# Convolution input in two DRAM tensors and started a group earlier, LayerNorm in four stages, attention's norm weight in the output weights

## The chip, the cores and the metric

The kernel runs on one core of a Trainium2 chip. The metric is the device time of one execution in microseconds (us), the median over runs.

## The reference

Two layers of a diffusion backbone over 256 prompt tokens and 1024 sample tokens (ten tiles of 128 tokens, width 1024). Each layer: RMSNorm with a modulation, one input projection, two branches of "heads", one output projection, a second RMSNorm, a gated residual. The change touches layer 0 alone (`even_mix`), of which this is the core:

```python
a_u, a_g, a_z, b_q, b_k, b_v, b_z = jnp.split(h @ w_in, SPLIT_E, axis=-1)
a = a_u * jax.nn.sigmoid(a_g)
a = lax.conv_general_dilated(a, conv_w[:, None, :], window_strides=(1,),
        padding=[(15, 15)], feature_group_count=A_W) + conv_b        # 512 channels, 31 taps
a = jax.nn.silu(layer_norm(a, ln_g, ln_b)) * jax.nn.silu(a_z)
...
o = over_query_blocks(lambda qb: diff_attend(qb, keys, vals, lam), q)  # softmax 1 - lam * softmax 2
o = rms_norm(o, subln_g) * (1.0 - lam_init)
o = o.reshape(b, T, B_W) * jax.nn.silu(b_z)
return jnp.concatenate([a, o], axis=-1) @ w_out, new_kv
```

## The kernel before, in words

**Layer 0's input part** (`l0_in`) is a list of seven groups of projections: ug0 and ug1 (each 256 channels of a_u and a_g), az, and head 0 to head 3 (q, k, v and z of one head of attention). A group has 10 units (one tile of tokens each) or, for a head, 14; TensorE does a unit as matmuls in three parts, of high and low halves, over eight chunks of weights `w_w`. In the last batch of a group (three or four units together) the next group's weights are loaded, cast on ScalarE (L269) and split on GpSimd (L270).

After every unit a `filler` advances a second piece of work by some steps: `cv`, which is the convolution followed by LayerNorm, and `mod`, the modulation vectors. Before, the groups from az on advance `cv` by one step a unit, and by two at every third. `cv` is a generator: `conv()` has 66 steps, which read the convolution's input back from DRAM in eight blocks of 64 channels (`windows`, tile `X`) and multiply it on TensorE by banded tap matrices (`band`; `tr_cv`, L471), with evictions on ScalarE (L476) and VectorE (L477); `ln_steps()` has six more, two tiles of tokens a step but for the first: load, statistics on VectorE (L574 to L581, with the root on GpSimd, L95), normalisation on ScalarE (L582) and GpSimd (L583, L584), tanh on ScalarE (L585), two multiplies on VectorE (L586, L587), store (L588). What is left of `cv` when the last group ends is run out after it.

In the heads, `ch_done` rotates q and k (sum on GpSimd L499, then L500 on ScalarE and L501 on VectorE), `vz_done` makes v and the gate `gz`: silu (L339, L340), then a multiply with `subg`, the norm weight of attention times 0.4 on every row (L513), and the store (L514). `split_stack` makes the prompt tokens' q and k (`hl`, L357; transposed on TensorE as `tr_st`, L360).

**Between input part and attention**, at a place in head 3 (`freed0`), keys of head 0 (`l0_keys`: loads `kd`, `ck`, subtractions on GpSimd L653) and the queries of its token group 1 (`l0_query`: `qs`, four loads) are loaded ahead.

**Attention** (`l0_attn`) takes for each head five groups of two tiles: scores S on TensorE (L777), row maximum and softmax (`row_softmax`: L394 on VectorE, the exponential L397 on ScalarE), two of them for each head. Their weighted difference: L784 and L785 make the weight `wc`, L787 (VectorE, first 1024 columns) and L789, L790 (GpSimd, the others) the difference E; then transposes, splits and the product with V. `fin` squares and sums the transposed output (L718 on ScalarE), adds the EPS term (L719, L720 on VectorE), takes the root (L95 on GpSimd) and multiplies by root and gate into `oy` (L724).

**Output projection**: `wo_chunk` loads a chunk of 128 rows of the output weights (`wor`, L815), casts it (ScalarE, L818) and splits it (GpSimd, L819); of eight chunks the last four belong to attention.

A scheduler puts the instructions in order when the kernel is built, by its own estimates; on the chip each engine then runs its list in that order, and the DMA issues of SP stand in one such list, too.

Of the kernel before, what the change touches and what calls it, by code (L numbers as in the profile page):

```python
# [76 lines left out]
class K:  # L77
# [323 lines left out]
    def l0_in(self, ws, raw, wp, cxp, p1, small, acc, pst, mod, freed):  # L401
# [4 lines left out]
        for hl in range(2):  # L406
            for r0, r1 in ((0, 15), (271, CW0 + 15), (CW0 + 15 + 1024, CROWS)):
                nc.sync.dma_start(f32(self.AW[hl, r0:r1]), z0[0 : r1 - r0])

        def ug_units(gi):  # L410
            def done(t, ps):
# [7 lines left out]
                dst = self.AW[:, r : r + 128, gi * 256 : gi * 256 + 256]  # L419
# [63 lines left out]
        def head_units(h):  # L483
# [23 lines left out]
            def vz_done(t, ps):  # L507
# [49 lines left out]
        def ln_steps():  # L557

            con = cxp.tile([128, 3, 512], F32, tag="cy", bufs=1, name="lncon")
            for i, nm in enumerate(("lng", "lnb", "convb")):  # L560
# [2 lines left out]
            def load(p):
                w = cxp.tile([128, CWIN * CCH], F32, tag="X", bufs=2, name=f"lu{p}")
                w = w[:, 0:2560].rearrange("p (i c) -> p i c", c=512)
                az = small.tile([128, 512], F32, tag="az", bufs=2, name=f"azr{p}")
                for i in range(2):
                    r = (2 * p + i) * 128 + (0 if p < 1 else CW0 - 256)
                    nc.sync.dma_start(w[:, i], self.CV[r : r + 128])
                    nc.sync.dma_start(w[:, 4] if i else az, self.AZ[2 * p + i])  # L570
                return w, (az, w[:, 4])

            def tile(t, u, th, az):
# [11 lines left out]
                nc.scalar.activation(th, u, AF.Tanh, scale=0.5)  # L585
                nc.vector.scalar_tensor_tensor(u, th, 1.0, u, ALU.add, ALU.mult)  # L586
# [974 lines left out]
```

## Time and profile before

| | |
|---|---|
| runs | 1823.73, 1828.43, 1829.55 us (median 1828.43) |
| the profiled execution | 1829.68 us, span 1827.9 us |
| mean granted TensorE clock | 0.985 |
| TensorE (PE) busy | 1727.2 us, 94% of the span |
| VectorE (DVE) | 1238.3 us, 68% |
| ScalarE (ACT) | 971.6 us, 53% |
| GpSimd (POOL) | 782.0 us, 43% |

The time is that of the whole execution; the span is from the first to the last instruction that the profiler saw. Busy shares are averages over stages with different limits. Layer 0's input part runs to some 514 us, its attention to some 800 us; layer 1 follows. In the page's 40 slices of 45.7 us TensorE's granted clock is 0.9 or more in all but one, which holds the passage from the input part to attention (0.7), and the DMA engines are 70 to 80% busy between 91 and 183 us and again from 229 to 411 us or so, with dips.

### The profile page before, as it was taken

The page shows a single profiled execution, that of the slowest core. Times are in us where ns is not written, and L with a number is a line of the kernel's source. Part 1 is how long each engine was busy: PE and PEld are TensorE (multiplying, and loading weights), DVE is VectorE, ACT ScalarE, POOL GpSimd, SP SyncE. Part 2 cuts the span into 40 slices and gives each one's busy share as a digit, 9 for nine tenths or more (in the row PEclk, how much of TensorE's full clock was granted, in tenths as well). Part 3 has the DMA queues.
Part 4 walks back from the last instruction along what each step waited for, and adds up shares of the span by engine and source line. Part 5 has one row for each costly group of instructions (what it writes and reads, how often), then busy time and mean ns, then how long its engine had stood idle before and what let it go on. Part 6 is the DMA issues. An engine that isn't in the chain of part 4 may idle for free. (4 is left out here: it accounts for less than half of the span.)

```text
span 1827.9 us, 28289 instructions
## 1 busy us (share of the span) xinstructions
PE 1727.2 (94%) x9434; PEld 1419.5 (78%) x9434; DVE 1238.3 (68%) x2975; ACT 971.6 (53%) x2040; POOL 782.0 (43%) x696
## 2 busy tenths in 40 slices
PE   6999999999859999899999999998999999999998
PEld 2787788988747777778887778886888888878886
DVE  6657545674779999945566672118899989999322
ACT  6432244344337777753344543217778878898311
POOL 2322022222557777763237873203344334354332
PEclk9999999999979999999999999999999999999999
DMA  8457478785764433144146346254112114141441
GB/s 292 166 161 211 150 185 203 190 234 134 222 185 113 139 104 93 47 137 163 72 156 199 139 121 167 75 137 113 36 43 66 36 41 107 53 146 58 156 173 55
DMA packets 220086, 241.24 MB, mean 132 GB/s; under 512 B 72128, under 2 KB 154464, under 8 KB 219684
## 3 DMA queue, kind: packets, MB, share of 16 engines
q1 hardware_dynamic: 207284, 233.53, 43.1%
q0 software_dynamic: 1792, 3.15, 0.9%
q10 hardware_dynamic: 10864, 2.75, 0.8%
q8 instruction: 75, 1.23, 0.3%
q14 instruction: 71, 0.58, 0.1%
HBM read 169.08 MB, written 70.28 MB: 131 GB/s over the span
## 5 line engine op out<-in xcount | busy, mean ns | idle before, releaser
L397 ACT ACTIVATE E<-E,mm 128x1536 f32<-128x1536 f32 (+3 forms) x240 | 293.5, 1227 | 69.0 <-DVE E L394 58.4
L270 POOL TENSOR_TENSOR w_w<-raw_w,w_w 128x512 fp32r<-128x512 f32 x88 | 118.7, 1360 | 258.1 <-ACT w_w L269 244.0
L1217 PE MATMUL S<-k1d,q1s 128*128 128x512 f32 (+1 forms) x704 | 206.4, 389 | 4.5 <-DMA q1s<-qT 2.1
L372 POOL TENSOR_TENSOR el<-ef,eh 128x512 fp32r<-128x512 f32 x96 | 124.3, 1296 | 185.6 <-DVE eh L371 180.7
L394 DVE TENSOR_SCALAR_CACHE_REDUCE E<-S,mm 128x512 f32<-128x512 f32 x256 | 189.8, 744 | 11.5 <-PE S L777 3.0
L1147 PE MATMUL wt_et<-ident,E 128*128 128x128 f32 x1264 | 186.2, 273 | 3.2 <-ACT E L397 2.5
L1147 PEld LDWEIGHTS wt_et<-ident,E 128*128 128x128 f32 x1264 | 153.6, 140 | 37.3 <-ACT E L397 4.3
L777 PE MATMUL S<-kd,qs 128*128 128x512 f32 (+1 forms) x416 | 133.4, 431 | 30.2 <-DVE E L394 24.1
L368 DVE TENSOR_TENSOR el<-wt_et,eh 128x512 fp32r<-128x512 f32 x220 | 146.8, 682 | 10.0 <-ACT eh L367 9.3
L1217 PEld LDWEIGHTS S<-k1d,q1s 128*128 128x128 f32 x704 | 121.3, 190 | 28.5 <-DVE E L394 7.1
L367 ACT CAST eh<-wt_et 128x512 fp32r<-128x512 f32 x220 | 124.1, 594 | 30.4 <-PE wt_et L1147 29.9
L1142 PE MATMUL pv_pv<-el,v 128*128 128x512 f32 x316 | 138.8, 439 | 0.5 <-POOL el L372 0.2
L318 PE MATMUL acc_g<-w_w,hi 128*128 128x512 f32 x336 | 131.5, 393 | 1.8 <-DVE v L1000 1.3
L319 PE MATMUL acc_g<-w_w,hi 128*128 128x512 f32 x336 | 132.4, 394 | 0.5 <-POOL w_w L270 0.5
L320 PE MATMUL acc_g<-w_w,lo 128*128 128x512 f32 x336 | 131.6, 392 | 0.0
L1141 PE MATMUL pv_pv<-eh,v 128*128 128x512 f32 x316 | 128.3, 406 | 0.9 <-DVE eh L371 0.5
L852 PE MATMUL acc_po<-wo,oh 128*128 128x512 f32 x320 | 126.0, 395 | 0.6 <-DVE oy L724 0.6
L853 PE MATMUL acc_po<-wo,oh 128*128 128x512 f32 x320 | 125.1, 392 | 0.0
L394 DVE TENSOR_SCALAR_CACHE_REDUCE E<-S 128x512 f32<-128x512 f32 (+1 forms) x160 | 99.8, 629 | 18.7 <-PE S L1217 11.7
L777 PEld LDWEIGHTS S<-kd,qs 128*128 128x128 f32 x416 | 70.0, 197 | 51.6 <-DVE E L394 38.6
L856 PE MATMUL acc_po<-wo,ol 128*128 128x512 f32 x320 | 103.3, 393 | 0.0
L269 ACT CAST w_w<-raw_w 128x512 fp32r<-128x512 f32 x96 | 59.0, 621 | 82.8 <-DMA raw_w<-in_wod 23.3
(294 smaller groups left out, 4544.4 us busy)
## 6 DMA issues: line engine op xcount, KB each, us to landing
rawm_v<-in_wmodt SPq DMA_DIRECT2D x64, 256.0 KB, 3.1
raw_w<-in_we SPq DMA_DIRECT2D x56, 256.0 KB, 3.4
X<-AW SPq DMA_DIRECT2D x32, 336.0 KB, 5.5
qs<-QK SPq DMA_DIRECT2D x80, 128.0 KB, 2.8
ac<-CAT SPq DMA_DIRECT2D x20, 512.0 KB, 3.5
raw_w<-in_wod SPq DMA_DIRECT2D x40, 256.0 KB, 2.8
q1s<-qT SPq DMA_DIRECT2D x40, 256.0 KB, 2.6
xraw_m<-in_wmod SPq DMA_DIRECT2D x32, 256.0 KB, 4.8
```

Source lines behind the costliest of these rows:

```text
L318: nc.tensor.matmul(ps[:, o:], a, w[:, 0, o:], start=(k == 0), stop=False)
L319: nc.tensor.matmul(ps[:, o:], a, w[:, 1, o:], start=False, stop=False)
L320: nc.tensor.matmul(ps[:, o:], b, w[:, 0, o:], start=False, stop=(k == KC - 1))
L368: nc.vector.tensor_tensor(lo, ps, f32(hi), ALU.subtract)
L394: nc.vector.tensor_scalar(e[:, o : o + w], S, -1.0, init, ALU.mult, ALU.min, accum_out=m[:, i : i + 1])
L397: nc.scalar.activation(e[:, :n], e[:, :n], AF.Exp, bias=init, scale=-1.0, accum_out=s)
L777: nc.tensor.matmul(S, q[:, hl], kd[:, c, kofs + o : kofs + o + n], start=(hl == 0), stop=(hl == 1))
L852: nc.tensor.matmul(po[hn], oh[:, k, :], wo[k][:, 0, s], start=(k == 0), stop=False)
L1141: nc.tensor.matmul(pv, vs, wh, start=(i == 0), stop=False)
L1142: nc.tensor.matmul(pv, vs, wl, start=False, stop=(i == nk - 1))
L1147: nc.tensor.transpose(ps[:, g * 128 : g * 128 + 128], E[g][:, ec : ec + 128], self.ident)
L1217: nc.tensor.matmul(S, qs[:, g, :], kd[hl][:, kc : kc + n], start=(hl == 0), stop=(hl == 1))
```

## The change

1. The convolution's input, one DRAM tensor `AW` of 512 channels, becomes two of 256, one for each ug group.
2. `filler` advances `cv` from ug1 on, at 4/3 of a step a unit while it convolves, and 0.8 in LayerNorm.
3. LayerNorm goes by single tiles in four stages (load, statistics, normalisation, tanh and gate) that are offset by steps, over six buffers cut from the two `X` tiles.
4. `subg` is not multiplied into `gz`; it becomes one column, and scales the rows of output chunks 4 to 7.
5. In `fin` the EPS term is made by a ScalarE square and added on GpSimd; `wc` takes the two-scalar form.
6. Queries of groups 1, 2 and 0 of head 0 are loaded ahead, with twelve loads in place of four.

```diff
@@ l0_in, ug_units and windows
-                dst = self.AW[:, r : r + 128, gi * 256 : gi * 256 + 256]
+                dst = self.AW[gi][:, r : r + 128]
...
-                        src = self.AW[hl, 32 * o : 32 * o + 32 * CWIN, cs].rearrange("(j r) c -> r j c", r=64)
+                        src = self.AW[q // 4][hl, 32 * o : 32 * o + 32 * CWIN, cs].rearrange("(j r) c -> r j c", r=64)
@@ vz_done
-                nc.vector.tensor_tensor(gz, gz, self.subg, ALU.mult)
@@ ln_steps
+            ws = [cxp.tile([128, CWIN * CCH], F32, tag="X", bufs=2, name=f"lnw{i}") for i in range(2)]
+            slots = [w[:, i * 512 : i * 512 + 512] for w in ws for i in range(5)]
+            us, azs, ths = slots[0:6], slots[6:8], slots[8:10]
...
-            for p in range(NT // 2):
-                w, az = nxt
-                if p + 1 < NT // 2:
-                    nxt = load(p + 1)
-                for i in range(2):
-                    tile(2 * p + i, w[:, i], w[:, 2 + i], az[i])
+            for s in range(NT + 3):
+                if s >= 3:
+                    gate(s - 3)
+                if s + 2 < NT:
+                    load(s + 2)
+                if 1 <= s <= NT:
+                    norm(s - 1)
+                if 2 <= s <= NT + 1:
+                    nc.scalar.activation(ths[s % 2], us[(s - 2) % 6], AF.Tanh, scale=0.5)
+                if s < NT:
+                    stats(s)
                 yield
+        convd, credit, RATE, LNR = [], [0.0], 4 / 3, 0.8
@@ filler
-                    n[0] += convs
-                    for _ in range(2 if convs and n[0] % 3 == 0 else convs):
+                    credit[0] += rate and (LNR if convd else rate)
+                    while credit[0] >= 1:
+                        credit[0] -= 1
                         next(cv, None)
@@ groups
-            (1, lambda: ug_units(1), tok, filler(0, 1)),
-            (6, az_units, tok, filler(1, 1)),
+            (1, lambda: ug_units(1), tok, filler(RATE, 1)),
+            (6, az_units, tok, filler(RATE, 1)),
...
@@ fin
+                nc.scalar.activation(ss[:, 2:4], sc[:, 0, :], AF.Square, scale=EPS ** 0.5)
...
-                    nc.scalar.activation(junk, ps[:, j * 128 : j * 128 + 128], AF.Square, accum_out=ss[:, j : j + 1])
-                nc.vector.scalar_tensor_tensor(ss[:, 2:4], sc[:, 0, :], EPS, sc[:, 0, :], ALU.mult, ALU.mult)
-                nc.vector.scalar_tensor_tensor(ss[:, 2:4], ss[:, 0:2], 1.0 / 128, ss[:, 2:4], ALU.mult, ALU.add)
+                    nc.scalar.activation(junk, ps[:, j * 128 : j * 128 + 128], AF.Square, scale=128.0 ** -0.5, accum_out=ss[:, j : j + 1])
+                nc.gpsimd.tensor_tensor(ss[:, 2:4], ss[:, 0:2], ss[:, 2:4], ALU.add)
@@ stage_a
-                qs = qs1 if (h, g) == (0, 1) else self.l0_query(h, g, at, 3)
+                qs = qs1[g] if h == 0 and g in qs1 else self.l0_query(h, g, at, 3)
...
-                    nc.vector.scalar_tensor_tensor(w[:, 1:2], sc[:, 0, j : j + 1], self.nlam, w[:, 0:1], ALU.mult, ALU.mult)
+                    nc.vector.tensor_scalar(w[:, 1:2], w[:, 0:1], sc[:, 0, j : j + 1], self.nlam, ALU.mult, ALU.mult)
@@ wo_chunk
+        if l == 0 and k >= 4:
+            nc.vector.tensor_scalar(r, r, self.subg, None, ALU.mult)
@@ freed0
-                pre.extend([[p], k.l0_keys(0, p, 1), k.l0_query(0, 1, p, 1)])
+                pre.extend([[p], k.l0_keys(0, p, 1), {g: k.l0_query(0, g, p, 3) for g in (1, 2, 0)}])
```

How the instructions of three engines stand, before and after. First VectorE, at the end of head 3; `lu` is LayerNorm's tile, `bn` and `mv` its statistics, `gz` the gate, E the softmax's result (E_1_0_0: group 1, tile 0, half 0). Before:

```order
L579 TENSOR_SCALAR mv_5061<-mv_5061 128x1
L581 TENSOR_SCALAR mv_5046<-mv_5046 128x1
L581 TENSOR_SCALAR mv_5061<-mv_5061 128x1
L586 SCALAR_TENSOR_TENSOR lu_4973<-lu_4973 128x512
L587 SCALAR_TENSOR_TENSOR lu_4973<-lu_4973,azr_4974 128x512
L586 SCALAR_TENSOR_TENSOR lu_4973<-lu_4973 128x512
L587 SCALAR_TENSOR_TENSOR lu_4973<-lu_4973 128x512
L394 TENSOR_SCALAR E_1_0_0_5504,mm_1_0_0_5514<-S_1_0_0_0_5505 128x512
```

And with the change, up to the same softmax:

```order
L357 TENSOR_TENSOR hl_1_0_5324<-nat_1_5289,hl_1_0_5324 128x4x64
L340 SCALAR_TENSOR_TENSOR gz_6_5338<-th_z_6_5339,acc_v_6_5299 128x128
L340 SCALAR_TENSOR_TENSOR gz_7_5371<-th_z_7_5372,acc_v_7_5343 128x128
L340 SCALAR_TENSOR_TENSOR gz_8_5404<-th_z_8_5405,acc_v_8_5376 128x128
L340 SCALAR_TENSOR_TENSOR gz_9_5437<-th_z_9_5438,acc_v_9_5409 128x128
L394 TENSOR_SCALAR E_1_0_0_5467,mm_1_0_0_5477<-S_1_0_0_0_5468 128x512
L394 TENSOR_SCALAR E_1_0_0_5467,mm_1_0_0_5477<-S_1_0_0_512_5471,mm_1_0_0_5477 128x512
L394 TENSOR_SCALAR E_1_0_1_5482,mm_1_0_1_5492<-S_1_0_1_0_5483 128x512
```

The LayerNorm rows between the last gate and the softmax are gone from there.

On SP, the loads of head 0's values, gate and queries. Before, from the last gate's store on, with LayerNorm's stores (CAT):

```order
L514 DMA GZ_71<-gz_9_5473 128x128
L588 DMA CAT_75<-lu_4973 128x512 x2
L743 DMA v_5495<-V_70 128x10x128
L744 DMA v_5495<-in_cbv 128x512
L752 DMA gzt_5501<-GZ_71 128x10x128
L661 DMA qs_2_5576<-QK_69 64x2x256 x4
L661 DMA qs_0_5620<-QK_69 64x2x256 x4
L646 DMA kd_5713<-QK_69 128x2x1280
```

With the change, in the middle of head 3:

```order
L667 DMA kd_5097<-QK_69 128x2x1280
L672 DMA ck_0_5101<-in_cbk 64x2x256
L682 DMA qs_1_5107<-QK_69 64x2x256 x4
L682 DMA qs_2_5112<-QK_69 64x2x256 x4
L682 DMA qs_0_5117<-QK_69 64x2x256
L672 DMA ck_1_5104<-in_cbk 64x2x256
L682 DMA qs_0_5117<-QK_69 64x2x256 x3
L594 DMA CAT_76<-lnw_4270 128x512 x2
```

The queries of groups 1, 2 and 0 now stand together with the first keys, ahead of LayerNorm's last stores, and 20 rows ahead of the load of V.

On GpSimd, the splits of head 3's weights (`w_w`). Before they stand one behind the other:

```order
L270 TENSOR_TENSOR w_w_0_4492<-raw_w_0_4486,w_w_0_4492 128x512
L270 TENSOR_TENSOR w_w_1_4509<-raw_w_1_4488,w_w_1_4509 128x512
L270 TENSOR_TENSOR w_w_2_4526<-raw_w_2_4490,w_w_2_4526 128x512
L270 TENSOR_TENSOR w_w_3_4557<-raw_w_3_4507,w_w_3_4557 128x512
L270 TENSOR_TENSOR w_w_4_4574<-raw_w_4_4524,w_w_4_4574 128x512
L270 TENSOR_TENSOR w_w_5_4613<-raw_w_5_4555,w_w_5_4613 128x512
L270 TENSOR_TENSOR w_w_6_4628<-raw_w_6_4572,w_w_6_4628 128x512
L270 TENSOR_TENSOR w_w_7_4655<-raw_w_7_4611,w_w_7_4655 128x512
```

With the change LayerNorm's multiplies and adds (`lnw`) and roots (`mv`) stand between them:

```order
L270 TENSOR_TENSOR w_w_0_4576<-raw_w_0_4570,w_w_0_4576 128x512
L587 TENSOR_TENSOR lnw_4270<-lnw_4270,lncon 128x512
L588 TENSOR_TENSOR lnw_4270<-lnw_4270,lncon 128x512
L270 TENSOR_TENSOR w_w_1_4593<-raw_w_1_4572,w_w_1_4593 128x512
L588 TENSOR_TENSOR lnw_4270<-lnw_4270,lncon 128x512
L270 TENSOR_TENSOR w_w_2_4610<-raw_w_2_4574,w_w_2_4610 128x512
L587 TENSOR_TENSOR lnw_4271<-lnw_4271,lncon 128x512
L588 TENSOR_TENSOR lnw_4270<-lnw_4270,lncon 128x512
L270 TENSOR_TENSOR w_w_3_4644<-raw_w_3_4591,w_w_3_4644 128x512
L270 TENSOR_TENSOR w_w_4_4661<-raw_w_4_4608,w_w_4_4661 128x512
L95 TENSOR_TENSOR mv_4725<-mv_4725,mhalf 128x1
L588 TENSOR_TENSOR lnw_4271<-lnw_4271,lncon 128x512
```

Three more splits follow, with five more LayerNorm operations among them. The multiplies and adds were all behind the eight splits before; seven of them are now within.

## Rows read from the trace of the kernel before

**Rows 1.** Table of stretches; columns: busy us of each engine, clock, DMA share, GB/s.

```profile
180.00:200.00 20.00, 19.89 (x90) 15.85 (x90) 12.86 (x33) 4.43 (x10) 1.14 (x1) 0.93 0.58 190
520.00:540.00 20.00, 6.93 (x18) 4.37 (x18) 12.84 (x32) 6.71 (x9) 8.56 (x9) 0.57 0.56 162
546.00:800.00 254.00, 233.98 (x1337) 189.32 (x1337) 235.99 (x619) 186.58 (x375) 188.12 (x148) 0.99 0.35 98
800.00:820.00 20.00, 18.48 (x86) 14.82 (x85) 2.06 (x5) 7.75 (x17) 11.21 (x10) 1.00 0.61 212
```

**Rows 2.** Timeline of TensorE (PE), 500 to 548; columns: start us, us, instruction.

```profile
500.90 1.12 PE L360 MATMUL tr_st<-ident,hl 128*128 128x128 f32 x4 [6.42 <-DVE hl L357]
...
502.03 0.41 PE L320 MATMUL acc_v<-w_w,lo 128*128 128x256 f32 x1
...
507.09 0.28 PE L320 MATMUL acc_v<-w_w,lo 128*128 128x256 f32 x1
...
508.38 0.28 PE L319 MATMUL acc_v<-w_w,hi 128*128 128x256 f32 x1
...
514.40 1.53 PE L777 MATMUL S<-kd,qs 128*128 128x512 f32 x6
532.92 7.23 PE L777 MATMUL S<-kd,qs 128*128 128x512 f32 x18 [16.99 <-DVE E L394]
545.32 0.77 PE L777 MATMUL S<-kd,qs 128*128 128x512 f32 x1 [5.16 <-DMA qs<-QK]
```

**Rows 3.** Timeline of VectorE (DVE), 475 to 550.

```profile
477.72 6.07 DVE L513 TENSOR_TENSOR gz<-gz,subg 128x128 f32<-128x128 f32 x1
...
520.10 1.37 DVE L574 SCALAR_TENSOR_TENSOR lu<-lu,lncon 128x512 f32<-128x512 f32 x2 [0.74 <-DMA lu<-CV]
...
529.13 1.07 DVE L586 SCALAR_TENSOR_TENSOR lu<-lu 128x512 f32<-128x512 f32 x1 [4.81 <-ACT lu L585]
...
532.18 0.68 DVE L394 TENSOR_SCALAR_CACHE_REDUCE E<-S 128x512 f32<-128x512 f32 x1
...
547.14 0.69 DVE L394 TENSOR_SCALAR_CACHE_REDUCE E<-S 128x512 f32<-128x512 f32 x1 [2.99 <-PE S L777]
```

**Rows 4.** Timeline of GpSimd (POOL), 470 to 536.

```profile
478.58 2.55 POOL L583 TENSOR_TENSOR lu<-lu,lncon 128x512 f32<-128x512 f32 x2
...
492.05 1.29 POOL L653 TENSOR_TENSOR kd<-ck,kd 64x512 fp32r<-64x512 f32 x1 [8.43 <-DMA qs<-QK]
```

**Rows 5.** Timeline of the DMA issuing queue (SP), 505 to 548.

```profile
532.70 0.39 SPq L743 DMA_DIRECT2D v<-V  x1
...
534.41 7.66 SPq L661 DMA_DIRECT2D qs<-QK  x8
```

**Rows 6.** Sources by line: count, ns min/median/max, first and last start.

```profile
L513 DVE TENSOR_TENSOR gz<-gz,subg x40: 254/291/6066, 259.9 to 519.1; 128x128 f32<-128x128 f32 x40
...
L719 DVE SCALAR_TENSOR_TENSOR oss<-sc x20: 147/377/1027, 543.6 to 789.7; 128x2 f32<-128x2 f32 x20
...
L720 DVE SCALAR_TENSOR_TENSOR oss<-oss x20: 134/150/1800, 574.0 to 802.6; 128x2 f32<-128x2 f32 x20
...
L785 DVE SCALAR_TENSOR_TENSOR wc<-sc,ls,wc x40: 204/218/1277, 540.9 to 787.4; 128x1 f32<-128x1 f32 x40
...
L95 POOL TENSOR_TENSOR oss<-oss,mhalf x20: 688/710/1664, 574.3 to 802.8; 128x2 f32<-128x2 f32 x20
...
L221 DVE TENSOR_SCALAR xr<-xr,ss_n x10: 745/753/1861, 834.1 to 941.2; 128x1024 f32<-128x1024 f32 x10
```

**Rows 7.** Waits of TensorE, 546 to 800: us in total, times, longest.

```profile
PE S L777 <- DVE E L394: 7.1, 13, 1.1
PE wt_wt L690 <- DVE E L787: 5.9, 9, 1.4
```

**Rows 8.** Waits of TensorE, 120 to 260.

```profile
PE tr_cv L471 <- DVE cy L477: 1.8, 1, 1.8
```

**Rows 9.** The page's DMA issues: count, KB each, us to landing.

```profile
X<-AW SPq DMA_DIRECT2D x32, 336.0 KB, 5.5
```

More of the change, by code (lines that the diff above doesn't have):

```diff
@@ L405, in l0_in @@
         nc.gpsimd.memset(z0, 0.0)
-        for hl in range(2):
+        for aw in self.AW:
             for r0, r1 in ((0, 15), (271, CW0 + 15), (CW0 + 15 + 1024, CROWS)):
-                nc.sync.dma_start(f32(self.AW[hl, r0:r1]), z0[0 : r1 - r0])
+                nc.sync.dma_start(f32(aw[:, r0:r1]).rearrange("a p c -> p a c"), z0[0 : r1 - r0].rearrange("p (a c) -> p a c", a=2))
         def ug_units(gi):
@@ L561, in ln_steps, with load, stats @@
                 nc.sync.dma_start(con[:, i], a[nm].broadcast_to([128, 512]))
[L563 to L566, printed above, removed]
-                for i in range(2):
[L568 to L573, printed above, removed]
+            ws = [cxp.tile([128, CWIN * CCH], F32, tag="X", bufs=2, name=f"lnw{i}") for i in range(2)]
+            slots = [w[:, i * 512 : i * 512 + 512] for w in ws for i in range(5)]
+            us, azs, ths = slots[0:6], slots[6:8], slots[8:10]
+            mvs = {}
+            def load(t):
+                r = t * 128 + (0 if t < NTP else CW0 - 256)
+                nc.sync.dma_start(us[t % 6], self.CV[r : r + 128])
+            def stats(t):
+                u = us[t % 6]
                 nc.vector.scalar_tensor_tensor(u, u, 0.5, con[:, 2], ALU.mult, ALU.add)
@@ L576, in tile @@
                 nc.vector.bn_stats(st, u)
-                mv = small.tile([128, 4], F32, tag="mv", name=f"mv{t}")
+                mvs[t] = mv = small.tile([128, 4], F32, tag="mv", bufs=3, name=f"mv{t}")
                 nc.vector.bn_aggr(mv[:, 0:2], st)
@@ L584, in tile, with gate @@
                 nc.gpsimd.tensor_tensor(u, u, con[:, 1], ALU.add)
[L585 to L587 removed]
+            def gate(t):
+                u = us[t % 6]
+                nc.vector.scalar_tensor_tensor(u, ths[t % 2], 1.0, u, ALU.add, ALU.mult)
+                nc.vector.scalar_tensor_tensor(u, u, 0.25, azs[t % 2], ALU.mult, ALU.mult)
                 nc.sync.dma_start(self.CAT[0][t, :, 0:512], u)
[L590 removed]
+            load(0)
             yield
[L592 to L597 removed]
+            load(1)
+            yield
+            yield
+            for s in range(NT + 3):
[9 more added lines that the diff above has]
+                    stats(s)
                 yield
+        convd, credit, RATE, LNR = [], [0.0], 4 / 3, 0.8
         def branch():
             yield from conv()
+            convd.append(True)
             yield from ln_steps()
@@ L605, in l0_in, with filler @@
         next(cv)
-        def filler(convs, mods, at=None):
-            left, n = [at], [0]
+        def filler(rate, mods, at=None):
+            left = [at]
             def f(b):
@@ L1242, in build @@
         k.AZ = dr.tile([NT, 128, 512], F32, name="AZ")
-        k.AW = dr.tile([2, CROWS, 512], F32R, name="AW")
+        k.AW = [dr.tile([2, CROWS, 256], F32R, name=f"AW{i}") for i in range(2)]
         k.CV = dr.tile([32 * CWIN, 512], F32, name="CV")
```

20 lines of the change are left out of this document (10 added, 10 removed).

## The prediction

> **What bounds the kernel now.** I read the profile from the whole to the place: first the table of 20 us stretches, then TensorE's own timeline where a stretch falls out, then the engine that ended each wait there.
>
> The stretches say that the kernel is bound by TensorE nearly everywhere, and at one seam by VectorE [rows 1]. Early in layer 0 (180 to 200) TensorE is busy 19.89 of 20 us. Attention of layer 0 (546 to 800) has it busy 233.98 of 254 us with VectorE at 235.99: two engines each with some 18 to 20 us free, neither alone the bound. Between them, from 520 to 540, TensorE works 6.93 us of 20 at a granted clock of 0.57. That is the passage from the last projection (head 3) to attention, and it is where the change works.
>
> TensorE's timeline names three waits in it [rows 2]. At 500.90 it has stood 6.42 us for `hl`, which VectorE makes. Then projection matmuls of one kind start 0.211 us apart (24 of them from 502.03 to 507.09), and after that 0.117 us apart (11 from 507.09 to 508.38): the lower granted clock after the stop costs 24 x 0.094 = 2.3 us. The last projections are followed at 514.40 by six score matmuls, and the next one runs at 532.92, after 16.99 us of waiting for the softmax on VectorE. At 545.32 it waits 5.16 us for query loads.
>
> VectorE's timeline tells what it did meanwhile [rows 3]. At 520.10 it starts the last pair of LayerNorm tiles, whose load had just come. It then waits 4.81 us for their tanh on ScalarE and multiplies by it from 529.13. Only at 532.18 does the first softmax operation (L394) run. The scores lay ready all that time: VectorE works in program order, and LayerNorm stood ahead. The 6.42 us have a similar root, further back: at 477.72 the multiply of `gz` by `subg` (L513) lasts 6.07 us. GpSimd runs two LayerNorm multiplies back to back inside that time [rows 4]. The `gz` store on the DMA issuing queue (SP) waits for that multiply, the cache key load `ck` stands behind it, GpSimd's key subtraction waits until 492.05 (8.43 us) for loads, and the rotary sum behind it starts at 493.42. Through that sum ScalarE and VectorE are late, and so is `hl`.
>
> **What the change costs and gives, part by part.**
>
> *The convolution starts one group earlier and LayerNorm ends before head 3's second half.* There are 66 convolution steps. At 4/3 of a step per unit they need 50 units: 10 of the second batch, 10 of az, 14 each of heads 0 and 1, and 2 of head 2. LayerNorm's 16 steps at 0.8 take 20 more, so they are over some 8 units into head 3, where they ran out behind its last unit before. The order confirms it: no LayerNorm row is left between head 3's last gate and the first softmax on VectorE. So the first softmax can start when the scores and the last gate are ready. The six score matmuls end at 514.40 + 1.53 = 515.9 [rows 2]; I allow 1.4 us for the tanh, the last gate and a store in front, so 517.3 in place of 532.18: **14.9 us**. At worst the GpSimd key subtractions, which stay late in the program, hold the scores back by a wait like that of 492.05: 8.4 us less.
>
> *The stall of 6.42 us goes.* The 40 multiplies L513 are removed, with the one of 6.07 us among them, and the LayerNorm multiplies on GpSimd no longer stand between the key loads and the rotary sum of head 3. **6.4 + 2.3 = 8.7 us**, the second being the slow clock that followed the stop. The other 39 are worth 0.29 us each [rows 6], and I count them at nothing, since TensorE carries that part and VectorE has room. From below: the same stop, for another late operand, gives nothing.
>
> *Three queries of head 0 are loaded ahead, not one.* Before, the loads of the other two start at 534.41 behind V [rows 5], and VectorE then waits 2.99 us for scores at 547.14 [rows 3]. They now stand on SP ahead of head 3's last stores: **3.0 us**. TensorE's 5.16 us there are the upper end, nothing the lower.
>
> *Attention's small operations.* VectorE loses L719 and L720, 20 each, whose medians are 0.377 and 0.150 us and whose longest are 1.03 and 1.80 [rows 6]: by the medians 10.5 us of VectorE. GpSimd gains 20 adds of the same 128x2 shape; the nearest row is the 0.710 us of its own 128x2 operation L95, so at most 14 us on an engine busy 188 of 254 us [rows 1]. ScalarE gains 20 squares of 128x2. L785 keeps its 0.22 us and only changes form. What of this is on the path? TensorE waited 7.1 us for softmax and 5.9 us for the weighted difference E there [rows 7], 13.0 us together. I take a little over half, **7 us**; the ends are 0 (TensorE at 234 of 254 us, held by something else next) and 13.
>
> *The output weights are scaled on VectorE*, four instructions of 128x1024. The nearest row is L221 of that shape, 0.753 us median and 1.861 longest [rows 6], so 3.0 to 7.4 us in all. VectorE works only 2.06 us from 800 to 820 [rows 1], so they are covered, except that each now stands between a weight's load and its split. The last chunk comes later by one of them: **1 us** lost, ends 0 and 4.
>
> The Trainium skill, "SBUF — State Buffer", section "Who interferes with whom", says that a VectorE instruction with two SBUF inputs contends with a GpSimd instruction that reads SBUF, and that the one that comes second blocks fully; L513's 6.07 us beside GpSimd's multiplies agrees. The same section says that `tensor_scalar` can contend as well, in its two-port modes, which speaks against this part of the change: scaling and GpSimd's splits of the same weights would block each other. By that rule, with L221's longest time for each of the four, the last weights come 4 x (1.861 - 0.753) = 4.4 us later and the sum below would be 26 us; by its median it stands.
>
> *The earlier convolution steps.* Some 26 of them now run in the second batch and az. There they compete with loads of weights; a wait of the kind at its first steps before is 1.8 us [rows 8], and an input load lands in 5.5 us [rows 9]. The steps are taken out of the later heads, where TensorE is as full, so the matmuls themselves cost nothing net. I set it to 0, ends 6 us either way.
>
> *LayerNorm in four stages, within heads 2 and 3.* The same arithmetic. New is that on GpSimd its multiplies stand among the eight splits (L270) of head 3's weights. Seven multiplies and adds there, at the 2.55 / 2 = 1.28 us of [rows 4], are 9 us put between them, and three roots besides. The splits go through during head 2's last batch of four units, chunk by chunk as TensorE frees each buffer, and most of the 9 us fit between two chunks: **2 us** lost, ends 0 and 8.
>
> The sum: 14.9 + 8.7 + 3.0 + 7 - 1 - 2 = 30.6 us. The profiled execution took 1829.7 us (its span 1827.9 and 1.8 around it), so 1799.1; it lies 1.3 us above the median of the runs, so I say **1798**.
>
> **The rivals.**
>
> 1. *The gain at the seam comes, and most is eaten nearby.* Weights of head 3 finish late on GpSimd (8 us), attention gives nothing for its VectorE (7 us less), since GpSimd's adds delay the gate that `oy` needs. 1798 + 6 + 7 = 1811. For it speaks that GpSimd is filled to three quarters; against it, that TensorE's waits for GpSimd in attention are few.
> 2. *More than the sum.* All 13 us of the waits in attention come back, the queries give 5.2, and the two losses are hidden: 1798 - 6 - 2.2 - 3 = 1787.
> 3. *Slower.* Each of the 26 early convolution steps waits for its input or band: TensorE and VectorE go through them in order, so one late step stops the projection behind it. At the 1.8 us of [rows 8] each that is 47 us, 1798 + 47 = 1845. It decides from 30.6 / 26 = 1.2 us a step on. DMA share there was already high in the profile's slices, which speaks for it. Against it: the first input was asked for in the second batch before, too, and up to 260 us the convolution steps of before made TensorE wait only that once.
> 4. *The change doesn't do what it says.* The softmax's path is free of LayerNorm by the order, but scores are late by the key subtractions, and another late `hl` holds the stack: then 8.4 of 14.9 and all 8.7 are missing, and with nothing from attention, 1798 + 8.4 + 8.7 + 7 = 1822. The same if conv steps and LayerNorm lag behind.
>
> **How the numbers follow.** Chances: forecast 0.58, its own range 1792 to 1806; rival 1 0.18; rival 2 0.13; rival 3 0.05; rival 4 0.06. The range takes the first two and the middle of the third, with part of the fourth, 1785 to 1814. A change under 0.3%, 5.5 us, about what a measurement of this kernel tells from none, means 1823 to 1834: half of rival 4 and a little of 3. Faster 0.92, same 0.04, slower 0.04.
>
> **What would show it right or wrong.** Right: in the profile after, no stop of TensorE near head 3's first stack; the first softmax within 3 us of the first scores; no wait for query loads behind it; clock near 1 in each stretch of the seam; VectorE's busy time in attention some 10 us lower, and TensorE's waits there about 6 instead of 13 us. Wrong: TensorE waits for `X`, `band` or a split weight in the second batch, az or at the start of head 3; or new waits for GpSimd before `oy`.

## The result and the profile after

The changed kernel takes 1840.74 us (median of 6 runs, 1836.14 to 1843.07) where the kernel before took 1830.25 us beside it (6 runs): a ratio of 1.0064, 95% interval 1.005 to 1.0078. The forecast was 32 us faster. The profiled execution took 1840.51 us at a mean granted clock of 0.984. Of x6 below, one execution at a clock of 0.557 (2825.35 us, the profiled one) is left out of its ratio, so x6 has no row in the table.

Cut at four instructions of TensorE's timeline (last projection matmul of layer 0, last output transpose of its attention, first `acc_g` matmul of layer 1, last `acc_po`), the two profiled executions, a second pair taken on another chip, and the experiments below that the argument uses compare so, in us:

| kernel | input part | attention 0 | of it to the first softmax | output 0 | layer 1 |
|---|---|---|---|---|---|
| before | 514.3 | 287.5 | 17.9 | 123.7 | 894.1 |
| changed | 531.4 | 273.7 | 1.5 | 124.6 | 900.6 |
| before, second pair | 519.4 | 287.3 | 18.1 | 123.8 | 895.2 |
| changed, second pair | 533.0 | 274.4 | 1.6 | 126.4 | 899.7 |
| x1, parts 4 to 6 alone | 523.1 | 290.9 | 19.0 | 124.4 | 898.9 |
| x2, parts 1 to 3 alone | 529.3 | 264.8 | 1.4 | 125.5 | 893.7 |
| x4, changed, tile padded | 532.0 | 275.1 | 1.0 | 124.2 | 895.3 |
| x5, changed, no queries ahead | 529.0 | 264.8 | 1.0 | 124.9 | 900.5 |
| x7, x4 and x5 together | 529.4 | 267.3 | 1.0 | 124.0 | 894.7 |
| x8, x7 and keys late | 534.1 | 261.7 | 3.2 | 124.2 | 895.5 |
| x9, x7 and LayerNorm late | 519.7 | 274.1 | 5.4 | 124.7 | 895.7 |
| x14, x2 and part 6 | 521.4 | 273.9 | 1.4 | 124.4 | 896.3 |
| x13, x2 and keys late | 520.5 | 267.7 | 3.6 | 123.0 | 896.1 |

The first pair adds up: 17.1 later at the last projection, 13.8 won in attention, 0.9 lost in the output projection, 6.5 in layer 1, together 10.7 us slower. The input part differs by some 5 us between two profiles of one kernel (514.3 and 519.4), so a single profile of it decides nothing under that; where a profile and the medians of many executions disagree below, the medians count.

The timeline of TensorE in the changed kernel, at its stops in heads 2 and 3 and the start of attention (answers to [rows 2]):

```profile
404.21 1.11 PE L360 MATMUL tr_st<-ident,hl 128*128 128x128 f32 x4 [2.75 <-DVE hl L357]
...
443.69 0.58 PE L318 MATMUL acc_v<-w_w,hi 128*128 128x256 f32 x1 [5.29 <-DVE gz L340]
...
468.24 0.80 PE L330 MATMUL acc_c<-hi,w_w 128*128 128x512 f32 x1 [5.52 <-ACT nat L526]
...
519.21 0.89 PE L360 MATMUL tr_st<-ident,hl 128*128 128x128 f32 x4 [4.97 <-DVE hl L357]
...
531.54 1.54 PE L798 MATMUL S<-kd,qs 128*128 128x512 f32 x6
533.72 1.61 PE L798 MATMUL S<-kd,qs 128*128 128x512 f32 x4 [0.63 <-DVE E L394]
```

The stop of 16.99 us ahead of the second scores is now 0.63 us. The stop for `hl` is still there, 4.97 us at 519.21. New are 5.29 us for a gate (`gz`) in head 2's last batch, 5.52 us for `nat` in front of head 3's first matmuls, and 2.75 us for `hl` of head 2. VectorE's timeline shows the first softmax:

```profile
532.97 0.68 DVE L394 TENSOR_SCALAR_CACHE_REDUCE E<-S 128x512 f32<-128x512 f32 x1
```

The table of stretches (answers to [rows 1]):

```profile
440.00:460.00 20.00, 16.31 (x84) 14.39 (x85) 11.99 (x23) 9.44 (x18) 20.00 (x16) 0.83 0.61 172
460.00:480.00 20.00, 14.48 (x68) 11.80 (x67) 17.08 (x29) 9.57 (x32) 17.85 (x14) 0.83 0.63 199
...
520.00:540.00 20.00, 16.68 (x106) 14.78 (x106) 5.70 (x18) 5.10 (x14) 1.19 (x2) 0.84 0.80 217
546.00:800.00 254.00, 230.09 (x1314) 187.42 (x1313) 229.98 (x583) 190.45 (x396) 195.27 (x169) 0.99 0.30 88
```

GpSimd is busy 20.00 of 20 us from 440 to 460, TensorE falls to 16.31 and 14.48 of 20 there with a granted clock of 0.83. In the same window of attention (546 to 800) VectorE's busy time fell from 235.99 to 229.98 us, 6 us where some 10 were forecast, and TensorE's did not rise: 230.09 in place of 233.98.

VectorE's timeline in head 2 and at the start of head 3 tells where the two new stops come from:

```profile
417.24 0.29 DVE L340 SCALAR_TENSOR_TENSOR gz<-th_z,acc_v 128x128 f32<-128x128 f32 x1 [0.93 <-ACT th_z L339]
429.07 0.69 DVE L574 SCALAR_TENSOR_TENSOR lnw<-lnw,lncon 128x512 f32<-128x512 f32 x1 [11.55 <-DMA lnw<-CV]
...
441.80 1.58 DVE L592 SCALAR_TENSOR_TENSOR lnw<-lnw,lnw 128x512 f32<-128x512 f32 x1
...
443.37 0.27 DVE L340 SCALAR_TENSOR_TENSOR gz<-th_z,acc_v 128x128 f32<-128x128 f32 x1
...
457.66 1.31 DVE L574 SCALAR_TENSOR_TENSOR lnw<-lnw,lncon 128x512 f32<-128x512 f32 x1 [5.39 <-DMA lnw<-CV]
...
467.32 0.28 DVE L340 SCALAR_TENSOR_TENSOR gz<-th_z,acc_p 128x128 f32<-128x128 f32 x1
```

After the gate at 417.24 its next instruction is the first LayerNorm statistic, and it stands 11.55 us for that tile's load. The gates and rotary products of the following units queue behind it, and what it has to make up holds `gz` until 443.37, when TensorE goes on. At 457.66 it stands 5.39 us for another such load, and TensorE goes on once the gate of 467.32 is made and `nat` read. From 441.8 on, most of its LayerNorm multiplies take more than twice what the shortest of them takes:

```profile
L592 DVE SCALAR_TENSOR_TENSOR lnw<-lnw,lnw x9: 680/1578/1784, 441.8 to 497.7; 128x512 f32<-128x512 f32 x9
```

The shortest of the nine is 0.680 us, the median 1.578. GpSimd runs without a pause beside them from 440 to 460. Seven of the nine start while a GpSimd instruction has over 0.1 us to run, and all seven end 0.55 us behind that instruction's end; the two others take 0.68 us. (The Trainium skill, "SBUF — State Buffer", section "Who interferes with whom", says that such two-input instructions and GpSimd's reads exclude each other; the rows agree.)

GpSimd's timeline, that of the DMA queue SP and VectorE's show where the stop for `hl` comes from:

```profile
511.93 1.29 POOL L674 TENSOR_TENSOR kd<-ck,kd 64x512 fp32r<-64x512 f32 x1 [15.56 <-DMA ck<-in_cbk]
513.29 2.51 POOL L499 TENSOR_TENSOR ch<-ch 128x512 f32<-128x512 f32 x2
```

```profile
505.07 0.61 SPq L672 DMA_DIRECT2D ck<-in_cbk  x1
505.73 7.30 SPq L682 DMA_DIRECT2D qs<-QK  x9
```

```profile
506.35 0.69 DVE L495 TENSOR_TENSOR ch<-cn,ropeT 128x512 f32<-128x512 f32 x1
```

The subtraction of head 0's cache keys stands 15.56 us for its key load, and the two rotary sums (L499) behind it wait with it, as before in [rows 4]. SP issues the load at 505.07, behind stores of head 3's keys, values and gates. No held multiply stands in this wait. Not all of the 15.56 us counts: the last products that the sums need are ready at 506.35 + 0.69 = 507.04, and the sums start at 513.29, so the key load makes them 6.3 us late, somewhat over the stop of 4.97. In the kernel before, by the rows of the same two engines, it was 3.3 us (490.17 to 493.42):

```profile
489.49 0.68 DVE L495 TENSOR_TENSOR ch<-cn,ropeT 128x512 f32<-128x512 f32 x1
```

```profile
493.42 2.50 POOL L499 TENSOR_TENSOR ch<-ch 128x512 f32<-128x512 f32 x2
```

### The profile page after: what moved, and what is told of

The parts are those of the page before. It is cut to its first block, busy times and chain, and to the rows that moved or that the text cites. A ratio compares the mean times of both kernels' runs of the same rounds, so it can differ in the third digit from the quotient of the medians.

```text
span 1838.7 us, 28232 instructions
## 1 busy us (share of the span) xinstructions
PE 1738.6 (95%) x9434; PEld 1425.9 (78%) x9434; DVE 1233.3 (67%) x2899; ACT 973.1 (53%) x2060; POOL 800.3 (44%) x716
## 3 DMA queue, kind: packets, MB, share of 16 engines
q10 hardware_dynamic: 10864, 2.75, 0.8%
## 4 chain that ended last, share of the span: by engine, by line
PE 57%; DVE 13%; DMA 8%; POOL 8%; issue 5%; SPq 2%; ACT 2%; DVEq 0%; POOLq 0%; ACTq 0%
PE S L1240 6%; PE wt_et L1170 6%; DVE E L394 4%; PE acc_po L879 4%; PE acc_po L876 4%; PE acc_po L875 4%; PE pv_pv L1165 3%; PE pv_pv L1164 3%; PE acc_g L318 3%; PE acc_g L320 3%; PE acc_g L319 3%; DMA rawm_v<-in_wmodt 2%; PE S L798 2%; DVE md_v L162 1%; PE acc_ug L318 1%
## 5 line engine op out<-in xcount | busy, mean ns | idle before, releaser
L270 POOL TENSOR_TENSOR w_w<-raw_w,w_w 128x512 fp32r<-128x512 f32 x88 | 126.9, 1451 | 239.8 <-ACT w_w L269 222.7
L372 POOL TENSOR_TENSOR el<-ef,eh 128x512 fp32r<-128x512 f32 x96 | 124.2, 1294 | 189.8 <-DVE eh L371 184.8
L394 DVE TENSOR_SCALAR_CACHE_REDUCE E<-S,mm 128x512 f32<-128x512 f32 x256 | 190.2, 745 | 14.9 <-PE S L798 6.3
L368 DVE TENSOR_TENSOR el<-wt_et,eh 128x512 fp32r<-128x512 f32 x220 | 147.2, 684 | 11.4 <-ACT eh L367 10.7
L367 ACT CAST eh<-wt_et 128x512 fp32r<-128x512 f32 x220 | 124.4, 595 | 31.7 <-PE wt_et L1170 31.2
L394 DVE TENSOR_SCALAR_CACHE_REDUCE E<-S 128x512 f32<-128x512 f32 (+1 forms) x160 | 100.3, 631 | 22.6 <-PE S L1240 12.9
```

What stands on the lines that cost most here:

```text
L394: nc.vector.tensor_scalar(e[:, o : o + w], S, -1.0, init, ALU.mult, ALU.min, accum_out=m[:, i : i + 1])
```

## The experiments

Two theories came out of the profile. A: the input part loses (parts 1 to 3, by the stops above). B: parts 5 and 6 lose.

**x0_before, x0_after**: both kernels unchanged, profiled on the chip of the next two.

> The kernel before, unchanged, for a profile on the chip of this group. Both theories: within 0.3% of the kernel before; a last projection matmul at about 514 us, a first softmax some 18 us behind it, and a pace of layer 1 that tells whether the 7 us which layer 1 seemed to lose are the chip's.

> The changed kernel, unchanged, for a profile on the same chip. Both theories: 0.4 to 0.8% slower than before. Theory A (the input part loses): last projection matmul 14 to 18 us later than in the kernel before, of it TensorE's waits in heads 2 and 3 some 18 us together; layer 1 takes as long as in the kernel before on this chip, within 2 us. Theory B (attention loses): the lag at the last projection is not steady, and attention from the first score to the last output is longer than the seam's gain allows by 8 us or more.

1835.78 and 1843.59 us. Layer 1 is 4.5 us longer in the changed kernel on the same chip, though its instructions are the same, in the same order on TensorE but for 27 of 4686 places: not the chip's pace.

**x1_attn_only and x2_input_only**: the change in two halves.

```diff
x1 = before + [ subg scaled into wor; fin; wc; queries (1, 2, 0) ahead ]
x2 = before + [ AW in two tensors; filler RATE 4/3, LNR 0.8; ln_steps in four stages ]
```

> The kernel before with parts 4, 5 and 6 of the change alone (norm weight in the output weights, EPS term on ScalarE and GpSimd, queries ahead); convolution, filler and LayerNorm as before. Theory A (the loss comes from the convolution and LayerNorm in heads 1 to 3, parts 1 to 3): faster than before by 3 to 10 us. Theory B (the loss comes from GpSimd's new adds and the query loads on the DMA issuing queue, parts 5 and 6): slower by 4 to 10 us, with the stall for hl longer than 6.4 us.

> The changed kernel with parts 4, 5 and 6 undone: the convolution from the second batch on and LayerNorm in four stages alone. Theory A: slower than before by 5 to 15 us, TensorE stalls of 5 us each near the end of head 2 and in head 3 as in the changed kernel. Theory B: faster than before by 5 to 15 us, since the first softmax no longer waits for LayerNorm.

x1: 1.0092 (1.0064 to 1.012). x2: 0.994 (0.9917 to 0.9962). Theory A falls. Parts 1 to 3 make the kernel 11 us faster although the stops come with them (x2 has stops of 5.5, 5.1 and 5.6 us, too): by the table the input part ends 9.9 us later than that of the second pair's kernel before, and attention is 22.5 us shorter. The other half costs 17 us, more than the 4 to 10 us that theory B expected. In x1 TensorE's timeline has the stop for `hl` at 10.31 us:

```profile
509.84 1.12 PE L360 MATMUL tr_st<-ident,hl 128*128 128x128 f32 x4 [10.31 <-DVE hl L357]
...
542.88 2.55 PE L776 MATMUL S<-kd,qs 128*128 128x512 f32 x5 [18.09 <-DVE E L394]
```

This stop has more than one root: in x1 the sums start only 1.5 us behind their products (497.64 and 499.14), and ahead of `hl` VectorE stands another 2.9 us for a LayerNorm load.

**x3 to x6**: what in that half costs.

```diff
x3  changed:  fin and wc as before (part 5 undone)
x4  changed:  k.subg = cst.tile([128, 128], F32, name="subg")[:, 0:1]
x5  changed:  pre.extend([[p], k.l0_keys(0, p, 1), k.l0_query(0, 1, p, 1)])    (part 6 undone)
x6  before: + k.dummy = cst.tile([128, 8], F32, name="dummy"); nc.gpsimd.memset(k.dummy, 0.0)
```

> The changed kernel with part 5 undone: the EPS term and the weight wc by VectorE's scalar_tensor_tensor as before, no added GpSimd adds. Theory G (the 20 GpSimd adds and ScalarE squares cost attention its gain): layer 0's attention, from the last projection to the last output, 6 to 10 us shorter than the changed kernel's 274, whole kernel 1.000 or faster. Theory P (the place of the tiles in SBUF, moved by the smaller norm weight tile, sets it): as the changed kernel, 1.005 to 1.008. Theory Q (the query loads ahead): as the changed kernel.

> The changed kernel with one thing more: the norm weight's tile keeps its old size of 128x128, of which one column is used, so that the tiles of layer 1 and of attention stand at their addresses of before; the instructions and their order are the same. Theory P: layer 1's projections and output projection at the pace of before (0.229 us a matmul in place of 0.232), some 6 us less behind layer 0, and attention of layer 0 shorter too if that depends on places: 0.996 to 1.001. Theories G and Q: as the changed kernel, 1.005 to 1.008.

> The changed kernel with part 6 undone: only one query block loaded ahead. Theory Q (nine query loads on the DMA issuing queue in head 3 hold up key loads, stores and so hl): the stall for hl near the end of head 3 shorter by 3 us or more, but query waits in attention come back (up to 5 us); 1.002 to 1.006. Theories G and P: 1.006 to 1.010, since the wait for queries returns and nothing is won.

> The kernel before with an unused constant tile of 32 bytes a partition behind the norm weight, so that the tiles of attention and layer 1 stand 32 bytes further; its order is the same. Theory P: slower than before by 5 to 12 us (1.003 to 1.007), with layer 1's matmuls at 0.231 to 0.233 us in place of 0.229. Theories G and Q: within 0.2% of before.

| | ratio to before | interval |
|---|---|---|
| x3 | 1.0069 | 1.0044 to 1.0095 |
| x4 | 1.0047 | 1.003 to 1.0064 |
| x5 | 1.0025 | 1.0009 to 1.0041 |
| x6 | 1.0036 | 1.0019 to 1.0054 |

Undoing part 5 in the changed kernel changes nothing (x3: 1.0069 beside 1.0064). The place of the tiles has a price: an unused 32 bytes a partition make the kernel before 0.36% slower. The old size of the tile gives the changed kernel 0.2% back, which is within the noise, and its 1.0047 misses the 1.001 or less that theory P expected; but layer 1 is then 895.3 us in place of 900.6. Every profile agrees on layer 1: 898.8 to 900.7 us in the five with the small tile (the changed kernel twice, x1, x3, x5), 892.7 to 897.7 in the twelve others but x6. The profile's groups of TensorE, changed kernel and then x4 (count, busy us, mean ns, idle before):

```profile
L319 PE MATMUL acc_g<-w_w,hi 128*128 128x512 f32 x336 | 133.3, 397 | 0.0
...
L876 PE MATMUL acc_po<-wo,oh 128*128 128x512 f32 x320 | 126.8, 396 | 0.0
```

```profile
L319 PE MATMUL acc_g<-w_w,hi 128*128 128x512 f32 x336 | 132.3, 394 | 0.4 <-POOL w_w L270 0.4
...
L876 PE MATMUL acc_po<-wo,oh 128*128 128x512 f32 x320 | 125.7, 393 | 0.0
```

The same 336 and 320 matmuls in the same order are each 3 ns shorter, and the output projection of layer 1, from the last score to its last matmul, takes 128.8 us in place of 131.0. x5 shows the queries: without the loads ahead the kernel is 0.4% faster and attention takes 264.8 us, not 274. Theory Q had the place wrong: the waits for `hl` are only 1.7 us shorter (7.7 to 6.0), not 3 or more.

**x7 to x10**: x7 is the changed kernel with x4's and x5's edits; on it, the stops of the input part one by one. Theory K is that the stop for `hl` comes from the wait of head 0's key subtraction on GpSimd; theory L, that the other two come from VectorE standing for LayerNorm loads.

```diff
x8   x7:  in l0_keys, for head 0, the GpSimd subtraction is issued after the two L499 sums;
          its key tile ck has two buffers in place of one (for heads 0 and 2)
x9   x7:  two more `yield` ahead of the first stats; the first six L574 after L495 of the last column group
x10  x7:  wcut(..., eng=nc.vector) for head 3's weights
```

> The changed kernel with the old size of the norm weight's tile and without the query loads ahead, both together. Theory A1 (the two costs found add, and parts 4 and 5 are worth nothing else): as the kernel with the input part alone, 0.993 to 0.997; attention of layer 0 264 to 266 us long, layer 1 894 to 896. Rival: the two fixes do not add, since the order of attention decides by luck: 0.998 to 1.003.

> The kernel x7 with GpSimd's subtraction of head 0's cache keys held back behind the rotary sums of head 3. Theory K (the stall of 5 us for hl near the end of head 3, in every kernel so far, comes from GpSimd waiting there for the key loads, with the sums queued behind): the stall goes, 5 to 8 us faster than x7. Rival (it comes from the held multiply of the gate, as the prediction had it): the multiply is gone already, the stall stays, within 2 us of x7.

> The kernel x7 with the first six LayerNorm statistics on VectorE held back behind the rotary multiplies of head 2's last column group, and two more empty steps in front of them. Theory L (TensorE's 5 us stop near the end of head 2 comes from VectorE standing 11 us at the first of them for its load, with the gates behind): that stop goes, 4 to 7 us faster than x7. Rival W (it comes from GpSimd, full with splits and LayerNorm): the stop stays or moves 5 to 10 us on, within 3 us of x7.

> The kernel x7 with the eight splits of head 3's weights on VectorE in place of GpSimd. Rival W (GpSimd, 20 of 20 us busy there, and what it holds up on VectorE cause the stops at the end of head 2 and the start of head 3): both stops get 3 us shorter or more, 4 to 10 us faster than x7. Theory L: the second stop may shrink, the first stays; within 3 us of x7, or slower since VectorE takes 5.5 us more there.

x7: 1.0005 (0.999 to 1.0019); x8: 0.9945 (0.9925 to 0.9964); x9: 0.9981 (0.9968 to 0.9994); x10: 0.9983 (0.9965 to 1.0). TensorE's waits from 120 to 560 us in each (us in total, times, longest), in the order x7, x8, x9, x10:

```profile
...
PE tr_st L360 <- DVE hl L357: 7.7, 2, 5.9
PE acc_v L318 <- DVE gz L340: 6.4, 2, 5.7
PE acc_c L330 <- ACT nat L526: 4.7, 1, 4.7
```

```profile
...
PE acc_c L330 <- ACT nat L526: 5.8, 1, 5.8
PE acc_v L318 <- DVE gz L340: 5.7, 1, 5.7
...
PE tr_st L360 <- DVE hl L357: 3.8, 3, 2.8
```

```profile
PE tr_st L361 <- DVE hl L358: 11.5, 3, 9.3
...
PE acc_v L319 <- DVE gz L341: 1.5, 1, 1.5
...
PE acc_c L331 <- ACT nat L527: 0.4, 1, 0.4
```

```profile
PE tr_st L361 <- DVE hl L358: 8.1, 3, 4.2
PE acc_v L319 <- DVE gz L341: 5.7, 1, 5.7
PE acc_c L333 <- DVE w_w L270: 3.2, 1, 3.2
```

x8 is 11 us faster than x7 (0.6% of 1830), more than the 5 to 8 expected, and its waits for `hl` halve: theory K holds. Two things stay open. x8 also gives the keys a second buffer, so that the second key load no longer waits for the first subtraction, and what that alone is worth was not tried. And the 11 us stand between the medians alone: the profiled execution of x8 is the slowest of its nine and that of x7 the fastest of its twelve, so the two traces are equally long. x9 takes both LayerNorm stops away (5.7 to 1.5, 4.7 to 0.4), so they came from VectorE standing for loads, as theory L says. It is 4 us faster than x7; at `hl` 3.8 us are given back (11.5 in place of 7.7), and in its profile attention is 6.8 us longer, 4.4 of them ahead of the first softmax. x10 leaves the first and shortens the second, and is 4 us faster than x7, which is within the noise: GpSimd's fullness is at most a part of the second. x7 missed its expectation: the two edits do add up (0.17% and 0.39% alone, 0.59% together), but parts 4 and 5 together still stand between it and x2.

**x11 to x14**, to settle that, and to price the queries and the keys on x2:

```diff
x11  x7:  part 5 undone           x13  x2:  keys late, two buffers, as in x8
x12  x7:  part 4 undone           x14  x2:  queries (1, 2, 0) ahead (part 6)
```

> The kernel x7 with part 5 undone (EPS term and wc on VectorE as before): the input part and part 4 with the tile padded. If part 5 costs what x7 lost against the input part alone: 0.993 to 0.996. If part 4 does: 0.999 to 1.002.

> The kernel x7 with part 4 undone (gz multiplied by the norm weight, output weights not scaled): the input part and part 5. If part 4 costs what x7 lost: 0.993 to 0.996. If part 5 does: 0.999 to 1.002. If both come out between, it is how often TensorE's clock falls, and neither edit has a price of its own.

> The input part alone with the key subtractions of head 0 held back behind head 3's rotary sums. If the stall for hl is worth there what it was on x7 (0.6%): 0.986 to 0.990, the fastest of all. If the two gains are one and the same (fewer falls of the clock): 0.992 to 0.996.

> The input part alone with part 6, queries of three groups loaded ahead, at the tile places of before. If the loads ahead cost what undoing them gave (7 to 10 us): 0.997 to 1.001, with attention of layer 0 8 to 11 us longer than the 265 us of the input part alone. If the prediction's price held: 2 to 4 us faster than the input part alone, 0.991 to 0.993.

x11: 0.9959 (0.9942 to 0.9976); x12: 0.993 (0.9907 to 0.9953); x13: 0.9903 (0.987 to 0.9935); x14: 0.9999 (0.998 to 1.0018).

Of parts 4 and 5 neither alone has a price clear of the noise: x2 has 0.994, with part 5 it has 0.993 (x12), with part 4 0.9959 (x11). With both it has 1.0005 (x7), 0.65% or 12 us more, and undoing either one gives most of it back (0.46% in x11, 0.75% in x12). So both expectations of x11 and x12 that lay the loss on one part came out, and the price is that of the two together. Its place was not found: the profiled execution of x7 is the fastest of its twelve, and beside x2's no stretch of it is more than 2.5 us longer. In the twelve executions of x7 the mean clock is 0.982 where x2 and x12 have 0.987 and x11 0.986, so the loss goes with longer time at the lower clock.

The queries ahead cost 0.6% on x2 (x14). In the two profiles attention is 9.1 us longer; x14's input part is 7.9 us shorter there, and its profiled execution is the fastest of its twelve, so the two profiles end only 2.5 us apart where the medians are 8 us apart. The table of stretches for attention, x14 and then x2:

```profile
521.40:795.30 273.90, 245.09 (x1370) 198.16 (x1368) 253.30 (x651) 196.76 (x390) 193.76 (x153) 0.98 0.37 99
```

```profile
529.30:794.10 264.80, 242.39 (x1371) 192.47 (x1370) 245.31 (x651) 195.47 (x390) 191.02 (x151) 0.99 0.38 104
```

With the same 651 instructions VectorE is busy 253.30 us in place of 245.31, 92 to 93% of the stretch in both, and TensorE 89 to 92%. VectorE's own longer work is 8 us, of 9.1 that the stretch is longer. x4 and x7, which differ by part 6 alone as well, agree: 1.0047 and 1.0005, attention 275.1 and 267.3 us, VectorE busy 242.53 and 233.74. (Queries are not all that sets attention's length: x9 has none ahead and 274.1 us, with VectorE busy 235.25.) Its groups in that stretch tell which (x14, then x2; count, busy us, mean ns, idle before):

```profile
L371 DVE CAST wh<-wf 128x512 fp32r<-128x512 f32 x32 | 23.5, 736 | 1.2 <-ACT wf L370 1.1
...
L742 DVE SCALAR_TENSOR_TENSOR oss<-oss 128x2 f32<-128x2 f32 x19 | 10.8, 570 | 0.0
```

```profile
L371 DVE CAST wh<-wf 128x512 fp32r<-128x512 f32 x32 | 19.9, 622 | 0.7 <-ACT wf L370 0.7
...
L742 DVE SCALAR_TENSOR_TENSOR oss<-oss 128x2 f32<-128x2 f32 x19 | 4.7, 245 | 0.1
```

L371 takes 114 ns more, 32 times (3.6 us), L742 325 ns more, 19 times (6.1 us); others gain and lose less. Both depend on GpSimd. Laid beside its timeline, the 11 L371 of x14 that run while GpSimd is idle (but for less than 0.1 us) take 0.42 us each, the 21 others 0.90 in the mean; of L742, 7 alone take 0.15 and 13 beside GpSimd 0.76. In x2 15 of L742 run alone and 5 beside it. One of the 21, with GpSimd's row:

```profile
600.46 1.40 DVE L371 CAST wh<-wf 128x512 fp32r<-128x512 f32 x1
```

```profile
600.29 1.28 POOL L376 TENSOR_TENSOR wl<-wf,wh 128x512 fp32r<-128x512 f32 x1
```

L376 ends at 601.57 and L371 at 601.86. Of the 19 L371 of x14 that start while a GpSimd instruction has over 0.1 us to run, 18 end 0.28 or 0.29 us behind that instruction, however long they last: they wait for its end. (The same section of the Trainium skill says that a cast in its two-port modes and an instruction with two SBUF inputs can be blocked by GpSimd; the rows agree.) So in the order built around the earlier loads these two meet GpSimd's work more often and longer. The changed kernel against x5 shows the same for L371:

```profile
L371 DVE CAST wh<-wf 128x512 fp32r<-128x512 f32 x32 | 28.8, 899 | 2.6 <-ACT wf L370 2.5
```

```profile
L371 DVE CAST wh<-wf 128x512 fp32r<-128x512 f32 x32 | 22.6, 707 | 4.4 <-ACT wf L370 4.4
```

6.2 us, beside the 8.9 that its attention is longer than that of x5 (273.7 to 264.8); VectorE's busy time over attention grows by 5.4 us (235.29 to 240.64). That VectorE's longer work makes attention longer is argued from these sums; no run held GpSimd off it. Why these meetings grow with that order was not traced further.

x13, 0.97% or 17.8 us under before, is the fastest of all; that it is 7 us faster than x2 is at the edge of the noise by itself, and 0.9903 lies just outside the 0.986 to 0.990 expected if the gain on x7 came back in full. Its GpSimd timeline has the sums ahead of the subtractions, and TensorE's wait for `hl` (120 to 560 us, x2 and then x13) falls from 5.6 to 1.4 us:

```profile
500.77 2.92 POOL L499 TENSOR_TENSOR ch<-ch 128x512 f32<-128x512 f32 x2 [10.63 <-DVE ch L494]
506.17 2.72 POOL L684 TENSOR_TENSOR kd<-ck,kd 64x512 fp32r<-64x512 f32 x2 [2.48 <-DMA ck<-in_cbk]
```

```profile
PE tr_st L360 <- DVE hl L357: 5.6, 1, 5.6
```

```profile
PE tr_st L360 <- DVE hl L357: 1.4, 1, 1.4
```

## Why the prediction was wrong

By the stretches of the table, the terms of the sum make the input part 6.7 us shorter, attention 24.9 shorter and the output projection 1 longer, and leave layer 1 alone. Measured in the two pairs of profiles, the input part is 13.6 to 17.1 us longer, attention 12.9 to 13.8 shorter, the output projection 0.9 to 2.6 longer and layer 1 4.5 to 6.5 longer. Term by term:

- *First softmax, 14.9 us*: right. It starts 1.5 us after the last projection in place of 17.9, 16.4 us won.
- *The stall of 6.42 us goes, 8.7 us*: wrong in its cause. The held multiply L513 is gone, and the stop is 4.97 us in the changed kernel. What makes it there is the link that the prediction named behind the multiply: the key subtraction, placed ahead of the rotary sums on GpSimd, stands for its load and makes the sums 6.3 us late. x8 and x13, which move it (and give the keys a second buffer), win 11 us on x7 and 7 us on x2. In the kernel before, the same link makes the sums 3.3 us late, a part of the 6.42; what L513 gave to that stop was not tried by itself. The fourth rival had this wait, and was given 6%.
- *Queries ahead, 3.0 us*: wrong in sign. The wait for them goes, but the kernel gets 0.4% (x5, and x7 against x4) to 0.6% (x14) slower, 7 to 11 us, and attention is 8 to 9 us longer in the profiles. With that goes, in the order built around the earlier loads, VectorE's longer work beside GpSimd (x14, x4, the changed kernel); that it is the cause is argued, not shown. The prediction looked at the order of SP alone, and at VectorE's medians, not at what stands beside each of its instructions on GpSimd.
- *Attention's small operations, 7 us*: VectorE lost 6 of the 10 us of busy time, and none of it reached the end: undoing part 5 changes nothing in the changed kernel (x3), adding it changes nothing on x2 (x12), and beside part 4 it costs 0.46% (x7 against x11). That is the lower end of the range given there, or below it.
- *Output weights, 1 us*: L838 takes 1.0 to 1.5 us, and the output projection is 0.9 us longer. What went unseen is the tile: from 512 to 4 bytes a partition, it moved all tiles behind it, and layer 1 became 4.5 to 6.5 us longer. Unseen, too, was that parts 4 and 5 together cost 12 us (x7 against x2), as much as the queries; where they cost it stays open.
- *LayerNorm in heads 2 and 3, 2 us*: mis-sized. Of the splits on GpSimd the prediction spoke; VectorE's stand at the first load and its making up cost two stops of 5.3 and 5.5 us. x9, which takes most of both away, is 4 us faster than x7.
- *Early convolution steps, 0*: about 2 us lost. TensorE waits 7.3 us for `cy` and `X` in the changed kernel, where it waited 1.8 for `cy` before; the 3.8 us for az's weights before are now 0.4.
- The third rival, slower by the early steps, had the right side and the wrong place. The DMA share that it leaned on was 50 to 70% from 91 to 183 us in the page's slices, not the 70 to 80% told ahead of the prediction.

Of the signs named, the first softmax did come within 3 us of the first scores (531.54 and 532.97); the stop near head 3's first stack stayed (4.97 us), and the granted clock from 520 to 540 is 0.84, not nearly 1.

Not settled: where the price of parts 4 and 5 together lies, why VectorE meets GpSimd more in the one order than in the other, and why the place of a tile changes a matmul's time.

## What to carry to other kernels

Where a scheduler sets the order, an edit that only loads something earlier changes the order of all that uses it: look at the order on the engine that is the bound, not on the queue of the load. Follow a chain of waits to the instruction that is waiting for memory while others queue behind it; a long instruction found on the way need not be what holds it, and of a long wait only the part counts by which the work behind it is late (6.3 of 15.56 us here). Run the halves of a change apart: here one gave 0.6%, the other took 0.9%. Two parts that cost nothing alone can cost together (parts 4 and 5, 0.65%), so undo them singly and jointly.

## What the runs showed of the hardware

Layer 1 ran the same instructions in the same order 5.3 us slower (900.6 us, x4 895.3) when a tile ahead of its own was 4 bytes a partition in place of 512, so that its tiles stood lower in SBUF, and the kernel before ran 0.36% slower with 32 unused bytes ahead of them; TensorE's matmuls took 397 ns in place of 394 in the groups shown. A VectorE copy of 128x512 (L371) took 0.42 us when GpSimd was idle and up to 2.48 us beside it, and a small operation of 128x2 (L742) 0.15 us and up to 1.81. Held ones ended a fixed time behind the GpSimd instruction that ran when they started: 0.28 us for L371 (x14, 18 of 19), 0.55 for the two-input multiply L592 (changed kernel, 7 of 7). So an engine with nearly 30% of its time free in a stretch (GpSimd in x14, busy 193.76 of 273.90 us) can still be the cause of another's longer time there.
